# A two-layer hybrid trunk on one core: one flag on the tile context, so that the list scheduler chooses every engine's order over another machine model

## The chip, the core and the metric

One core of a Trainium2 chip runs the whole kernel. Its engines have a queue of instructions each and work through it strictly in the order in which the program puts them there: PE (TensorE, matrix products), DVE (VectorE), ACT (ScalarE), POOL (GpSimd) and SP (which here only issues DMAs). An instruction whose operands or whose target buffer are not ready holds up everything behind it on the same engine. The metric is device time in microseconds (us): the median of several executions.

## The reference, cut to what is computed

528 positions (512 and 16 learned ones ahead of them) of width 1024 pass two layers. Each layer has a token mixer and a gated feed-forward part with a short convolution, and a LayerNorm behind each of the four. The first mixer is a gated delta rule over 8 heads of width 128, in chunks:

```python
for i in range(DEPTH):                       # DEPTH = 2
    if i % 2 == 0:
        mix = gated_deltanet(h, ...)         # 8 heads, chunked
    else:
        mix = short_conv_mixer(h, ...)
    h = layer_norm(ALPHA * h + mix, ...)
    h = layer_norm(ALPHA * h + conv_ffn(h, ...), ...)

# inside gated_deltanet, for each head
u = solve(I + m, v_beta)                     # lower triangular, m from k, beta, decay
w = solve(I + m, k_beta * exp(g))
for each chunk i:                            # a chain from chunk to chunk
    v_new = u_i - w_i @ state
    o_i = qg_i @ state + qk_i @ v_new
    state = state * exp(gl_i) + kd_i.T @ v_new
```

## The kernel before

Everything is float32 and held transposed: `h` is 128 partitions by 8 strips by 528 positions. A large product is made of three products of rounded halves, high with high, high with low, low with high; the halves are called `hh`/`hl` for the activations and `wh`/`wl` for the weights:

```python
TE.matmul(ps, hi[:, k, :], r_h, ...)         # L278
TE.matmul(ps, hi[:, k, :], r_l, ...)         # L279
TE.matmul(ps, lo[:, k, :], r_h, ...)         # L280
```

The halves are made by `split`: ACT writes the high one (L88), DVE subtracts for the low one (L89). Weights come by DMA into `raw` tiles and are split just ahead of their use.

**The first stage (to about 380 us) is the gated delta rule.** It has two kinds of work on PE:

- *Projections* from `hh`/`hl` and the weights, lines L278 to L280: `psba` (decay and beta), `ps<head><group><half>` (k, v and q of a head, 144 matmuls for a head) and `psz<head><half>` (the output gate, 48 for a head). They hang on nothing but weights and a free buffer. ACT takes their results out of PSUM (L416/L417, or L624 for the gate), and DVE and ACT make the convolution and the activation; the buffers of these results are few (two PSUM banks, three or four tiles of each kind), so a projection can run ahead of the heads only so far.
- *The heads' own chains* of small dependent matmuls. `gdn_a` (L444 ff.) makes for each head transposes and products (`pk`, `pv`, `pn`, `pp`, `pq`, `psNb`), and then seven levels of a triangular inverse. A level is `p1` on PE (L508), ACT to `T` (L513), `p2` on PE (L519), DVE into `D` (L520), `pt` on PE (L524), ACT to `DT` (L525), and the next level's `p1`. Level 0 has no `p2`. `pr` (L534/L535), `pz` (L543/L544) and `py` (L550) refine the inverse. `gdn_b` is the recurrence over five chunks: `sa` on PE (L571), ACT to `vn` (L572), `sa` on PE (L575), DVE to the state `St` (L577/L579), `sa` and `sb` on PE (L566, L567), DVE to `rr` (L568), and L571 again. Then `po0` and `po` (L588, L585), a norm on ACT, DVE and POOL (L595 to L600), and `gdn_c`'s transpose `pot` (L610), after which the head's strip of `h` is ready.

Names such as `p263` are read as `p2`, head 6, level 3; `sa7` is head 7's recurrence. Two or three heads are in flight at once (recurrence of head i, levels of heads i+1 and i+2). The first product behind the stage is `pd0`, and it needs all of `h`, that is `pot7`.

**Behind it** come `down(0)` with a LayerNorm, the first feed-forward part (`ffn(1)`: `up`, `pairs`, `down(1)`), the short convolution (`short_conv`, with `down(2)`), the second feed-forward part and the final norm. A LayerNorm inside `down` goes in two halves of positions, because of what PE can do meanwhile: the first half's products `pd_<m>_0` come first, some of the second half's (`pd_<m>_1`) are held back, and the norm of the first half is to run beside them:

```python
for m in range(2, KD):
    together(go(m, 0))
    if m < keep:
        together(go(m, 1))
lnorm(idx, *rng[0], acc[0])
for m in range(keep, KD):
    together(go(m, 1))
lnorm(idx, *rng[1], acc[1])
```

In `lnorm` PE makes `mean` (L711), DVE subtracts it (L715), ACT squares (L717, L720), DVE adds (L721), PE makes `var` (L722), ACT a reciprocal root `r0` (L724), DVE refines it (L725 to L727) and multiplies (L732), ACT writes `hh` (L733) and `h` (L734), DVE `hl` (L735). The next products `pu` need `hh` and, one step on, `hl`. `var1_12` and `mean1_272` are of `down(1)`: its first half begins at position 12, its second at 272.

**What sets the order.** The code hands its instructions to the tile framework in an order that `weave` (L648), `staggered` and the held-back products lay out by hand. When the context closes, the framework's list scheduler goes through them with a model of the machine, and puts on each engine's queue what that model says is ready and first; it also decides there in which order buffers of one kind are given out, and so which semaphores an instruction waits for. Nothing else in the kernel fixes the order. The context is opened at L1207.

## Time and profile before

| | |
|---|---|
| median of 3 executions | 1331.18 us (1330.91 to 1331.32) |
| the profiled execution | 1330.96 us |
| its span on the core | 1329.2 us, so 1.8 us lie around it |
| granted TensorE clock, mean | 0.999 |
| matmuls in the profile, all engines' instructions | 10569, 26094 |
| first `pd0` (end of the first stage) | 379.69 us from the span's start |

A row of a window gives for each engine the time it was busy in that stretch and, after x, the number of instructions. A row of a timeline gives the start, the duration, the engine, the line, and the operation with its tiles (without their numbers); what stands in brackets is the idle time just before it and what ended it. Matmuls are pipelined, so the distance from one start to the next, and not the duration, is what a matmul costs on a full queue.

### The profile page before, as it was taken

To read this page: it belongs to the slowest core of one execution; us is meant where nothing else is said; L and a number is where in the kernel's file an instruction comes from. 1 tells how busy PE (TensorE), PEld (TensorE's weight loads), DVE (VectorE), ACT (ScalarE), POOL (GpSimd) and SP (SyncE) were. 2 spreads that over 40 slices of the span, in tenths; PEclk is the share of its full clock that TensorE was granted. 3 is DMA by queue.
4 is the path that set the end of the run, shared out by engine and by line. 5 is a ranking of instruction groups with operands and counts; after the bars stand their busy time and mean duration, and the time that the engine had idled before them with its cause. 6 is when DMAs were issued, how large, how long until landed. Compare 5 with 4: busy or idle time off the path is not lost.

```text
span 1329.2 us, 26094 instructions
## 1 busy us (share of the span) xinstructions
PE 1295.3 (97%) x10569; PEld 1244.6 (94%) x10569; DVE 1039.4 (78%) x1875; ACT 765.6 (58%) x1597; POOL 91.8 (7%) x132
## 2 busy tenths in 40 slices
PE   7999999999999999999999999999999999999997
PEld 6899989999999999999999999999998998998996
DVE  6667777776567898968959789889689796895987
ACT  5676767776454846626636566456377562662660
POOL 0322333311010000000000000000000000000000
PEclk9999999999999999999999999999999999999999
DMA  5111111111161142522422511423133242341331
GB/s 201 64 49 33 49 48 33 49 37 45 49 209 62 38 138 81 152 71 77 147 64 89 151 49 60 132 96 125 51 96 112 64 143 80 96 143 49 97 126 63
DMA packets 36185, 116.87 MB, mean 88 GB/s; under 512 B 4065, under 2 KB 5601, under 8 KB 36065
## 3 DMA queue, kind: packets, MB, share of 16 engines
q1 hardware_dynamic: 35280, 112.83, 27.4%
q0 software_dynamic: 640, 2.12, 0.5%
q8 instruction: 82, 1.34, 0.4%
q14 instruction: 39, 0.31, 0.1%
q10 hardware_dynamic: 144, 0.26, 0.1%
HBM read 113.10 MB, written 2.10 MB: 87 GB/s over the span
## 4 chain that ended last, share of the span: by engine, by line
PE 81%; DVE 10%; ACT 4%; issue 2%; POOL 2%; DMA 1%; SPq 0%; DVEq 0%; ACTq 0%; POOLq 0%
PE px L278 6%; PE px L280 6%; PE px L279 6%; PE pd L278 5%; PE pd L279 5%; PE pd L280 5%; PE pz L278 3%; PE pz L279 3%; PE pz L280 3%; PE pt L822 3%; PE pt L823 3%; PE pt L824 3%; PE pu L280 2%; PE pu L279 2%; PE pu L278 2%; PE ps L280 2%
## 5 line engine op out<-in xcount | busy, mean ns | idle before, releaser
L88 ACT ACTIVATE wh<-raw 128x512 fp32r<-128x512 f32 (+3 forms) x309 | 234.9, 767 | 187.5 <-PE pd L279 60.8
L89 DVE TENSOR_TENSOR wl<-raw,wh 128x512 fp32r<-128x512 f32 (+3 forms) x309 | 263.2, 862 | 60.9 <-ACT wh L88 60.0
L88 ACT ACTIVATE wh<-s 128x512 fp32r<-128x512 f32 x129 | 81.3, 630 | 100.1 <-PE pt L823 45.3
L278 PE MATMUL pd<-gh,wh 128*128 128x260 f32 (+2 forms) x480 | 135.5, 284 | 2.0 <-ACT gh L88 1.2
L279 PE MATMUL pd<-gl,wh 128*128 128x260 f32 (+2 forms) x480 | 135.4, 283 | 0.0
L280 PE MATMUL pd<-gh,wl 128*128 128x260 f32 (+2 forms) x480 | 134.9, 282 | 0.0
L279 PE MATMUL pu<-hl,wh 128*128 128x258 f32 (+3 forms) x400 | 114.4, 289 | 1.5 <-DVE hl L735 1.4
L278 PE MATMUL ps<-hh,wh 128*128 128x264 f32 x384 | 114.5, 299 | 0.9 <-ACT acc L417 0.9
L280 PE MATMUL ps<-hh,wl 128*128 128x264 f32 x384 | 115.3, 300 | 0.0
L279 PE MATMUL ps<-hl,wh 128*128 128x264 f32 x384 | 114.1, 297 | 0.0
L280 PE MATMUL pu<-hh,wl 128*128 128x258 f32 (+3 forms) x400 | 113.3, 288 | 0.5 <-DVE wl L89 0.5
L278 PE MATMUL pu<-hh,wh 128*128 128x258 f32 (+3 forms) x400 | 113.2, 288 | 0.0
L89 DVE TENSOR_TENSOR wl<-s,wh 128x512 fp32r<-128x512 f32 x129 | 88.7, 687 | 12.4 <-ACT wh L88 9.4
L278 PE MATMUL px<-sumh,wh 128*128 128x258 f32 (+1 forms) x344 | 97.6, 284 | 0.0
L280 PE MATMUL px<-sumh,wl 128*128 128x258 f32 (+1 forms) x344 | 97.5, 283 | 0.0
L278 PE MATMUL px<-hh,wh 128*128 128x258 f32 (+1 forms) x344 | 97.3, 283 | 0.0
L279 PE MATMUL px<-suml,wh 128*128 128x258 f32 (+1 forms) x344 | 97.3, 283 | 0.0
L280 PE MATMUL px<-hh,wl 128*128 128x258 f32 (+1 forms) x344 | 96.9, 282 | 0.0
L279 PE MATMUL px<-hl,wh 128*128 128x258 f32 (+1 forms) x344 | 96.9, 282 | 0.0
L278 PEld LDWEIGHTS pd<-gh,wh 128*128 128x128 f32 x480 | 90.1, 188 | 2.8 <-ACT gh L88 1.4
L279 PEld LDWEIGHTS pd<-gl,wh 128*128 128x128 f32 x480 | 90.5, 189 | 0.4
L280 PEld LDWEIGHTS pd<-gh,wl 128*128 128x128 f32 x480 | 90.5, 189 | 0.0
(315 smaller groups left out, 4098.3 us busy)
## 6 DMA issues: line engine op xcount, KB each, us to landing
raw<-in_w_up_dram SPq DMA_DIRECT2D x88, 512.0 KB, 3.7
raw<-in_w_bi_dram SPq DMA_DIRECT2D x24, 512.0 KB, 3.8
raw<-in_w_qkv_dram SPq DMA_DIRECT2D x23, 512.0 KB, 3.7
raw<-in_w_dt_dram SPq DMA_DIRECT2D x22, 512.0 KB, 4.5
raw<-in_w_dn_dram SPq DMA_DIRECT2D x24, 384.0 KB, 3.5
raw<-in_w_z_dram SPq DMA_DIRECT2D x8, 512.0 KB, 3.7
raw<-in_w_ao_dram SPq DMA_DIRECT2D x8, 512.0 KB, 3.7
raw<-in_w_bo_dram SPq DMA_DIRECT2D x8, 384.0 KB, 3.5
```

The source lines that it names most:

```text
L88: S.activation(hi, src, AF.Copy)
L89: V.tensor_tensor(lo, src, hi.bitcast(F32), ALU.subtract)
L278: TE.matmul(ps, hi[:, k, :], r_h, start=start and k == 0, stop=False, **kw)
L279: TE.matmul(ps, hi[:, k, :], r_l, start=False, stop=False, **kw)
L280: TE.matmul(ps, lo[:, k, :], r_h, start=False, stop=stop and k == nk - 1, **kw)
L822: TE.matmul(ps, gh[:, k, ts_], w_h, start=k == 0, stop=False)
L823: TE.matmul(ps, gl[:, k, ts_], w_h, start=False, stop=False)
L824: TE.matmul(ps, gh[:, k, ts_], w_l, start=False, stop=k == nk - 1)
```

## The change

```diff
--- before.py
+++ after.py
@@ -1204,7 +1204,7 @@
-    with tile.TileContext(nc) as tc:
+    with tile.TileContext(nc, schedule_with_timeline_sim=True) as tc:
         tile_hybrid_trunk(tc, *args)
```

The list scheduler now runs over its other model of the machine, the one that has engine queues. The instructions that compute and the DMAs are the same ones; the order on the queues and the waits differ. On PE 8251 of 11274 instructions stand at another place: up to 1086 places away in the first stage, about 100 at most behind it. The queue that issues the DMAs moves by five places or fewer. ACT has 415 instructions that only wait for semaphores where there were 348, PE 33 where there were 24.

The first place is PE's queue in the middle of head 7's recurrence, `sa7`, near the end of the first stage. Before:

```order
L571 MATMUL sa7_4446<-rr7_4445,DT7_3961 106x128
L279 MATMUL psz40_4754<-hl_69,wh0_82 128x260
L280 MATMUL psz40_4754<-hh_68,wl0_83 128x260
L278 MATMUL psz41_4780<-hh_68,wh0_82 128x258
L279 MATMUL psz41_4780<-hl_69,wh0_82 128x258
L575 MATMUL sa7_4446<-vn7_4442,kd7_3962 128x128
L280 MATMUL psz41_4780<-hh_68,wl0_83 128x258
L278 MATMUL psz41_4780<-hh_68,wh0_82 128x258
L279 MATMUL psz41_4780<-hl_69,wh0_82 128x258
L280 MATMUL psz41_4780<-hh_68,wl0_83 128x258
L278 MATMUL psz41_4780<-hh_68,wh0_82 128x258
L566 MATMUL sa7_4446<-St7_4444,qkv7_1_3740 106x128
```

The same queue now, from the first `sa7` on:

```order
L571 MATMUL sa7_4446<-vb7_3963,DT7_3961 106x128
L575 MATMUL sa7_4446<-vn7_4442,kd7_3962 128x128
L610 MATMUL pot6_4459<-cst_sb_71,oS6_4256 128x106 x5
L566 MATMUL sa7_4446<-St7_4444,qkv7_1_3740 106x128
L567 MATMUL sb7_4447<-St7_4444,qkv7_0_3738 106x128
L571 MATMUL sa7_4446<-rr7_4445,DT7_3961 106x128
L575 MATMUL sa7_4446<-vn7_4442,kd7_3962 128x128
L566 MATMUL sa7_4446<-St7_4444,qkv7_1_3740 106x128
L567 MATMUL sb7_4447<-St7_4444,qkv7_0_3738 106x128
L571 MATMUL sa7_4446<-rr7_4445,DT7_3961 106x128
L575 MATMUL sa7_4446<-vn7_4442,kd7_3962 128x128
```

The gate's projections that stood between the links of the chain have moved ahead of it, and the links stand one behind the other.

The second place is PE's queue at the variance of the first half in `down(1)`. Before, `var1_12` stands in the middle of a held-back strip (`pd1_4_1`), with the rest of it and strips 5 to 7 of the second half behind it:

```order
L280 MATMUL pd1_4_1_98_9753<-gh_5023,wl0_83 128x256
L278 MATMUL pd1_4_1_98_9753<-gh_5023,wh0_82 128x256
L722 MATMUL var1_12_9620<-acc1_0_9419,onesm_76 128x260
L279 MATMUL pd1_4_1_98_9753<-gl_5024,wh0_82 128x256
L280 MATMUL pd1_4_1_98_9753<-gh_5023,wl0_83 128x256
```

Now it stands behind the last held-back strip, `pd1_7_1`, with the mean of the second half and the next stage's products right behind it:

```order
L279 MATMUL pd1_7_1_98_9816<-gl_5024,wh1_5015 128x256
L280 MATMUL pd1_7_1_98_9816<-gh_5023,wl1_5016 128x256
L722 MATMUL var1_12_9620<-acc1_0_9419,onesm_76 128x260
L711 MATMUL mean1_272_9837<-acc1_1_9420,onesm_76 128x256
L278 MATMUL pu99_0_0_9929<-hh_68,wh1_5015 128x258
L278 MATMUL pu100_1_0_9933<-hh_68,wh1_5015 128x258
```

The variance has moved behind all of the second half's products, and nothing but the second mean stands between it and the products that need the norm.

The third place is ACT's queue at the same norm, behind its reciprocal root `r01_12`. Before:

```order
L724 ACTIVATE r01_12_9652<-var1_12_9620,epsc_132 128x260
L88 ACTIVATE wh0_82<-raw120_9490 128x1024
L88 ACTIVATE wh0_82<-raw121_9911 128x1024
L733 ACTIVATE hh_68<-h_67,par_sb_70 128x260 x2
L734 ACTIVATE h_67<-h_67,par_sb_70 128x260 x2
```

And now:

```order
L724 ACTIVATE r01_12_9652<-var1_12_9620,epsc_132 128x260
L717 ACTIVATE acc1_1_9420<-h_67 128x256
L720 ACTIVATE s2_1_272_1_9843<-h_67 128x256
L720 ACTIVATE s2_1_272_2_9847<-h_67 128x256
L720 ACTIVATE s2_1_272_3_9851<-h_67 128x256
L720 ACTIVATE s2_1_272_4_9855<-h_67 128x256
L720 ACTIVATE s2_1_272_5_9859<-h_67 128x256
L733 ACTIVATE hh_68<-h_67,par_sb_70 128x260 x2
```

The second half's squares have moved ahead of the first half's output; on DVE the subtractions that feed them (L715, eight of them) stand ahead of L732 in the same way. `down(0)` and `down(2)` show the same three moves.

## The prediction

> **What bounds the kernel now.** I read the page first, for the shares and the chain of work that ended last:
>
> ```profile
> span 1329.2 us, 26094 instructions
> PE 1295.3 (97%) x10569; PEld 1244.6 (94%) x10569; DVE 1039.4 (78%) x1875; ACT 765.6 (58%) x1597; POOL 91.8 (7%) x132
> PE 81%; DVE 10%; ACT 4%; issue 2%; POOL 2%; DMA 1%; SPq 0%; DVEq 0%; ACTq 0%; POOLq 0%
> ```
>
> PE is busy for 97% of the span, and four fifths of the chain lie on it. The change adds and removes no instruction that computes, so it can gain only from PE's gaps, and lose wherever it opens new ones. The busy time by windows says where the gaps are:
>
> ```profile
> 0.00:33.00 33.00, 24.14 (x165) 20.87 (x166) 20.55 (x58) 18.35 (x35) 2.50 (x23) 1.00 0.59 202
> 200.00:300.00 100.00, 96.32 (x943) 91.60 (x941) 73.66 (x128) 72.83 (x196) 26.48 (x27) 1.00 0.15 43
> 300.00:380.00 80.00, 76.30 (x701) 72.10 (x701) 45.00 (x82) 43.03 (x114) 8.52 (x9) 1.00 0.17 49
> 500.00:600.00 100.00, 100.00 (x834) 99.76 (x834) 80.97 (x138) 52.66 (x97) 0.00 (x0) 1.00 0.32 98
> 782.00:802.00 20.00, 19.60 (x161) 19.30 (x160) 18.37 (x47) 13.01 (x28) 0.00 (x0) 1.00 0.36 110
> ```
>
> The first figure behind the length is PE. Behind the first stage it has no gap (500 to 600: 834 matmuls, 0.12 us each). In the first stage it loses under 4%, though there it runs chains of small dependent matmuls. At a LayerNorm (782 to 802) it loses 0.4 of 20 us. PE's waits, grouped by what ended them, are short:
>
> ```profile
> PE psba L278 <- ACT hh L88: 7.4, 2, 4.8
> PE sa L566 <- DVE St L579: 3.0, 4, 1.0
> PE pot L610 <- DVE oS L600: 2.5, 2, 1.5
> ```
>
> The largest is the start. The dependent steps wait little because projections stand between them, as the rows of the first place in the section on the change show. So the question is what happens to each dependent step when the order changes.
>
> **What a dependent step costs when nothing covers it.** From PE's timeline near the end of the first stage:
>
> ```profile
> 335.19 0.41 PE L508 MATMUL p<-D,N 106*106 106x106 f16 x5
> 336.37 0.41 PE L519 MATMUL p<-T,DT 106*106 106x106 f16 x5
> 337.58 0.44 PE L524 MATMUL pt<-ident,D 106*106 106x106 f16 x5
> 338.73 0.21 PE L534 MATMUL pr<-D,N 106*106 106x106 f16 x1
> 341.36 0.25 PE L543 MATMUL pz<-DT,N 106*106 106x106 f16 x1
> 342.48 0.28 PE L280 MATMUL psz<-hh,wl 128*128 128x258 f32 x1
> 342.94 0.21 PE L543 MATMUL pz<-DT,N 106*106 106x106 f16 x1
> 342.99 0.21 PE L544 MATMUL pz<-DT,L 106*106 106x106 f16 x1
> 343.02 0.37 PE L278 MATMUL psz<-hh,wh 128*128 128x258 f32 x1
> 343.22 0.28 PE L279 MATMUL psz<-hl,wh 128*128 128x258 f32 x1
> 347.15 0.41 PE L571 MATMUL sa<-vb,DT 106*106 106x128 f32 x2
> 354.70 0.49 PE L575 MATMUL sa<-vn,kd 106*128 106x128 f32 x2
> 355.62 0.47 PE L566 MATMUL sa<-St,qkv 128*106 128x128 f32 x2
> 356.54 0.47 PE L571 MATMUL sa<-rr,DT 106*106 106x128 f32 x2
> 357.46 0.49 PE L575 MATMUL sa<-vn,kd 106*128 106x128 f32 x2
> 361.02 0.38 PE L588 MATMUL po<-vn,PT 106*106 106x128 f32 x2
> 361.27 1.12 PE L585 MATMUL po<-vn,PT 106*106 106x128 f32 x8
> 367.58 0.67 PE L610 MATMUL pot<-cst_sb,oS 106*128 106x106 f32 x5 [1.48 <-DVE oS L600]
> ```
>
> These are head 7's last steps. A **level step** (L508, L519, L524, L534) comes 1.15 to 1.21 us after the one before: 1.2. A **recurrence step** (L575, L566, L571, L575) comes every 0.92. From `pr` to the first `sa` there are 8.42 us with projections put between; taking those out I choose 7 (estimate; the two shortest of its three gaps, 2.6 and 1.3, stay). From `po0` to `pot` there are 6.56. On the engine itself a half-precision matmul costs 0.05 (342.94 to 342.99), a float32 one about 0.2 (four in 361.27's 1.12, less its tail), and a projection 0.12, the first behind small ones 0.20 (343.02 to 343.22), so a break costs 0.05 to 0.08.
>
> **The first stage, term by term.** PE's new queue up to `pot7` holds the same 1584 projection matmuls and 1464 small ones, but the projections stand in 81 runs where there were 229, and all of them stand ahead of `pot7` (90 stood behind it). They run far ahead: 864 are queued, to head 5's v strip `ps521`, before head 0's level 5. Then they are held by their buffers, and the queue has long stretches of small matmuls alone. I cut it in stretches with projections (F) and without (E).
>
> The seven F stretches: 1584 × 0.122 = 193, their 425 small matmuls 49 at the prices above, 74 breaks × 0.05 = 4. The first 33 us stay as they are: 165 matmuls that would take 20 take 33, so 13 more. Sum **259**; these stretches wait for nothing.
>
> The E stretches run at the pace of their chains. Where a level of one head and a recurrence step of another alternate in the queue, as they do nearly everywhere, both go at the slower one's 1.2:
>
> - E1 (`pt04` to `po00`): 7 level steps 8.4, `pr` to `sa` 7, 12 recurrence steps 14.4: 29.8
> - E2 (in head 1's recurrence, up to `ps600`): 8 steps, 9.6
> - E3 (`pt26` to `po02`): 1.2 + 7 + 14.4 = 22.6
> - E4 (two pieces around `psz50`/`psz51`): 5, and 3 steps with `pr` to `sa` 10.6: 15.6
> - E5 (`sa4` to `po05`): 21 recurrence steps 25.2, and some 6 for eight groups of five float32 matmuls among them: 31
> - E6 (`pt65` to `pot7`): 4 steps 4.8, 7, 14.4 for `sa6`, 3.4 from `po06` to `sa7`, 12 × 0.92 = 11 for `sa7` alone, 1 for `po`, 6.6: 48.2
>
> That is 157. The same prices make 25.6 of before's stretch from 338.73 to 367.58 (7 + 11 + 1 + 6.6), which took 28.85, 1.13 times as long. I take 157 × 1.13 = 177. The stage then ends at 259 + 177 = 436 instead of 379.7: **+56**. The lower bound has each recurrence at 0.92 throughout and no 1.13: 65 steps × 0.28 = 18 less, 139, so +18. For the upper bound two chains that share a queue wait for each other's ACT and DVE work as well; 1.3 times 157 is 204, so +83.
>
> **The three LayerNorms in `down`.** Before, at the second:
>
> ```profile
> 777.94 0.60 PE L722 MATMUL var<-acc,onesm 128*128 128x260 f32 x2
> 782.12 0.41 DVE L756 TENSOR_TENSOR h<-h,pd 128x256 f32<-128x256 f32 x1
> 782.45 0.42 DVE L727 SCALAR_TENSOR_TENSOR r<-s,r 128x260 f32<-128x260 f32 x1
> 784.28 1.09 ACT L733 ACTIVATE hh<-h,par_sb 128x260 fp32r<-128x260 f32 x2
> 785.23 0.28 PE L280 MATMUL pd<-gh,wl 128*128 128x256 f32 x1
> 785.35 0.63 PE L278 MATMUL pu<-hh,wh 128*128 128x258 f32 x4
> 786.38 0.39 PE L279 MATMUL pu<-hl,wh 128*128 128x258 f32 x1 [0.40 <-DVE hl L735]
> ```
>
> From `var` to the first `pu` go 7.41 us, and held-back `pd` fill them to 785.23. In the new order nothing is left for that (second place of the change). Counted from the last `pd`: DVE adds it to `h` and closes the sums, five instructions 0.34 apart and a hop, so `var` at 2.3; the root `r0` done at 3.3 behind a `var` and an ACTIVATE; then 13 DVE instructions to L732 (L725 to L727, two L721, and the eight L715 of the other half), 4.4, so 7.8; `hh` one L732 and one ACTIVATE (0.55 of the pair's 1.09) later, at 8.7; `hl` behind eight L732 and an L721, at 11.3. PE has the two norm matmuls and six `pu` to do in that, about 1.3: **10 us idle at each, +30**. Lower bound: the 7.41 of before less a mean matmul's 0.6, 6.8 each, +20. Upper: DVE also has one or two splits of weights there (1.2 each in the same timeline), 12.7 each, +38.
>
> **The rest.** Behind the first stage nothing else moves more than about 100 places on PE, and I found two places where a matmul stands closer to its producer than before (in the first strip of `down(0)`, and at `ph1`): 3, between 0 and 8. The DMA queue moves by five places or fewer, and DMA is busy 15 to 36% of the windows above behind the start: 0. The 67 added waits on ACT stand on work that the E stretches already count.
>
> Sum: 1331 + 56 + 30 + 3 = **1420 us**. The profiled execution's 1330.96 is 0.2 under the median, which changes nothing.
>
> [...] The startup shows PE at another pace:
>
> ```profile
> 10.34 0.40 PE L278 MATMUL psba<-hh,ba_hi 128*16 128x264 f32 x1 [2.59 <-ACT hh L88]
> 14.74 0.42 PE L280 MATMUL ps<-hh,wl 128*128 128x264 f32 x1
> 14.96 0.42 PE L278 MATMUL psba<-hh,ba_hi 128*16 128x264 f32 x1
> 15.69 0.28 PE L280 MATMUL psba<-hh,ba_lo 128*16 128x264 f32 x1
> ```
>
> Behind the idle time the matmuls start 0.22 apart until 15 us, then 0.12, while the granted clock of that window is shown as 1.00. [...]
>
> **The rivals.**
>
> - *The slow pace of the start comes back* where PE is thin. For it: PE's own work in the E stretches (1039 small matmuls at the prices above) is 101 of 177 us, and the rows of the start. Against it: no gap inside an E stretch is longer than some 2 us. Price: at 0.22 for 0.12 that work takes 0.83 × 101 = 84 more, of which waits hide some 30, with 5 behind the norms: 1420 + 59 = 1479. [...] Chance 0.15.
> - *The chains go at their bare prices*, and DVE and ACT, free of projections, are early: +18 to +25 and +20 at the norms, so 1370 to 1378. For it: ACT and DVE are below 75% in the stage. Chance 0.2.
> - *Not slower.* 148 fewer breaks × 0.05 to 0.08 gain 7 to 12 us, already in my sum. If the chains of two or three heads hid each other, so that the E stretches took PE's own work of 101, the stage would end at 360 and gain 20; with norms that cost 7 in all, 1331 − 20 + 7 = 1318. It decides if the E stretches take less than 380 − 259 − 7 = 114 us in all, 13 more than PE's own work. Against it: the last `sa7` steps have nothing beside them, and their chain alone takes 19 us (11 + 1 + 6.6) for some 4 of work. Chance 0.04.
> - That nothing changes is excluded by the two orders.
>
> **How the numbers follow.** Forecast 1395 to 1450, chance 0.55; the rest (0.06) is worse than 1485. The range 1370 to 1485 takes both bounds of the two large terms (1331 + 18 + 20 = 1369; 1331 + 83 + 38 + 8 = 1460, and the slow pace above it). About 0.2%, 2.7 us, is what a measurement of this kernel can tell from no change. Faster by more than that 0.04, within 0.02, slower 0.94.
>
> **What would show it.** PE's busy share in the windows of the first stage falls from 96% to below 80% between 140 and 420 us, and stays near 96% ahead of 138; the first `pd0` starts near 436. New PE waits of the kind "`sa` L575 for ACT `vn`", "`p` L519 for ACT `T`", "`pt` L524 for DVE `D`" sum to 60 us or more. Three idles near 10 us stand ahead of `pu` (waiting for `hh` L733 and `hl` L735), and the windows away from them hold 834 matmuls in 100 us as before. Projections 0.22 apart in F stretches would show the slow pace. The forecast is wrong if the busy share of the first stage stays above 90%, or if `var` at the norms doesn't stand idle before the next `pu`.

## The result: 1453 us, 9.1% slower

| | before | after |
|---|---|---|
| median | 1331.25 us (1330.91 to 1332.26, 4 runs) | 1453.17 us (1450.79 to 1454.75, 4 runs) |
| ratio | | 1.0914 (95% interval 1.0901 to 1.0927) |
| span of the profiled execution | 1329.2 us | 1451.1 us |
| first `pd0`, end of the first stage | 379.7 us | 460.3 us |
| from there to the end of the span | 949.5 us | 990.8 us |
| mean granted TensorE clock | 0.999 | 0.942 |

The forecast was 1420 us in a range of 1370 to 1485. Of the 121.9 us that the span grew, 80.6 lie in the first stage and 41.3 behind it. The page of the changed kernel, its first lines and the rows of PE and its granted clock in 40 slices:

```profile
span 1451.1 us, 26169 instructions
PE 1347.8 (93%) x10569; PEld 1287.9 (89%) x10569; DVE 1047.1 (72%) x1875; ACT 773.1 (53%) x1597; POOL 86.7 (6%) x132
PE   7999888998777979999999997999979999999997
PEclk9999897998955989999999998999979999999999
```

DVE and ACT are busy for as long as before to within 1%, so the work is the same; PE, with as many matmuls, is busy for 52 us longer and still only 93% of the span. The clock row says how both can be: in before every slice had a 9, and here eight slices are lower: five in the first stage (slices 5 to 13, down to 5) and one at each of the three LayerNorms in `down` (slices 15, 25 and 30). PE's waits, grouped by what ended them (us in total, times, longest):

```profile
PE pu L278 <- ACT hh L733: 15.9, 3, 5.6
PE var L722 <- DVE acc L721: 11.2, 3, 4.8
PE p L519 <- ACT T L513: 5.7, 14, 0.8
PE pt L524 <- DVE D L520: 5.5, 11, 1.2
PE p L508 <- ACT DT L525: 4.9, 10, 1.5
PE sa L575 <- ACT vn L572: 3.3, 7, 0.7
```

The first two are the three norms, 27 us. The others are links of the heads' chains, which hardly waited before. Stretches of the first stage, as the prediction cut them (E1, F2, E3, E5, E6; PE's busy time and count first, the granted clock behind POOL):

```profile
134.80:171.90 37.10, 29.38 (x265) 25.12 (x262) 21.01 (x40) 23.38 (x55) 9.45 (x13) 0.77 0.05 15
171.90:195.40 23.50, 23.44 (x214) 23.44 (x215) 15.49 (x27) 13.15 (x42) 3.87 (x6) 1.00 0.16 46
233.90:266.50 32.60, 25.63 (x205) 22.19 (x205) 17.41 (x33) 19.45 (x49) 10.02 (x13) 0.74 0.06 17
352.50:389.80 37.30, 29.87 (x280) 24.95 (x279) 26.51 (x54) 20.68 (x71) 8.29 (x8) 1.00 0.06 15
396.20:460.30 64.10, 45.34 (x265) 36.36 (x263) 26.11 (x50) 24.92 (x64) 8.38 (x11) 0.54 0.12 38
```

F2 is full: 23.44 of 23.5 us. The E stretches hold 265 matmuls in 37 us or in 64, and in all of these but E5 the clock is down. Head 7's recurrence lies in the last of them; PE's timeline shows one of its chunks:

```profile
443.63 0.79 PE L575 MATMUL sa<-vn,kd 106*128 106x128 f32 x2 [0.46 <-ACT vn L572]
444.86 0.76 PE L566 MATMUL sa<-St,qkv 128*106 128x128 f32 x2 [0.44 <-DVE St L579]
446.06 0.76 PE L571 MATMUL sa<-rr,DT 106*106 106x128 f32 x2
447.28 0.80 PE L575 MATMUL sa<-vn,kd 106*128 106x128 f32 x2 [0.46 <-ACT vn L572]
```

It takes 3.65 us, where before's took 2.76 with projections between its links, and each row of two matmuls lasts 0.76 to 0.80 where it lasted 0.47 to 0.49.

### The profile page after: what moved, and what is told of

The parts are those of the page before. It is cut to its first block, busy times and chain, and to the rows that moved or that the text cites. A ratio compares the mean times of both kernels' runs of the same rounds, so it can differ in the third digit from the quotient of the medians.

```text
span 1451.1 us, 26169 instructions
## 1 busy us (share of the span) xinstructions
PE 1347.8 (93%) x10569; PEld 1287.9 (89%) x10569; DVE 1047.1 (72%) x1875; ACT 773.1 (53%) x1597; POOL 86.7 (6%) x132
## 4 chain that ended last, share of the span: by engine, by line
PE 84%; DVE 7%; ACT 5%; issue 2%; DMA 1%; POOL 0%; SPq 0%; DVEq 0%; ACTq 0%; POOLq 0%
PE px L280 6%; PE px L279 6%; PE px L278 6%; PE pd L278 5%; PE pd L279 5%; PE pd L280 5%; PE pu L279 4%; PE pu L280 4%; PE pu L278 3%; PE ps L278 3%; PE ps L280 3%; PE ps L279 3%; PE pz L280 3%; PE pz L278 3%; PE pz L279 3%; PE pt L822 3%
## 5 line engine op out<-in xcount | busy, mean ns | idle before, releaser
L278 PE MATMUL pd<-gh,wh 128*128 128x260 f32 (+2 forms) x480 | 130.3, 282 | 3.0 <-ACT gh L88 3.0
L278 PE MATMUL pu<-hh,wh 128*128 128x258 f32 (+3 forms) x400 | 113.6, 301 | 15.9 <-ACT hh L733 15.9
L279 PE MATMUL pu<-hl,wh 128*128 128x258 f32 (+3 forms) x400 | 118.9, 298 | 2.3 <-DVE hl L735 2.3
L280 PE MATMUL pu<-hh,wl 128*128 128x258 f32 (+3 forms) x400 | 117.7, 295 | 0.0
L88 ACT ACTIVATE wh<-s 128x512 fp32r<-128x512 f32 x129 | 80.7, 626 | 68.6 <-PE pd L279 22.8
L280 PE MATMUL ps<-hh,wl 128*128 128x264 f32 x384 | 111.1, 290 | 0.0
L279 PE MATMUL ps<-hl,wh 128*128 128x264 f32 x384 | 110.7, 289 | 0.0
L278 PEld LDWEIGHTS pu<-hh,wh 128*128 128x128 f32 x400 | 76.7, 201 | 18.5 <-ACT hh L733 17.8
```

What stands on the lines that cost most here:

```text
L88: S.activation(hi, src, AF.Copy)
L278: TE.matmul(ps, hi[:, k, :], r_h, start=start and k == 0, stop=False, **kw)
L279: TE.matmul(ps, hi[:, k, :], r_l, start=False, stop=False, **kw)
L280: TE.matmul(ps, lo[:, k, :], r_h, start=False, stop=stop and k == nk - 1, **kw)
```

## The experiments

Where nothing else is said, each starts from the changed kernel. An edge between two instructions below orders them on their engine's queue and makes neither wait for the other's end. The scheduler chooses everything that has no edge anew, so each run has its own orders on the other queues too. `behind` gives such edges to all instructions of the same engine traced since a mark:

```python
def behind(tc, n0, ins):
    for i in traced(tc)[n0:]:
        if i.engine == ins.engine:
            tc.add_manual_dep(i, ins.name, ORDER, reason="order")   # ORDER: NoSync
```

| run | median us | end of the first stage | from `mean` of `down(1)`'s first half to its `pu` |
|---|---|---|---|
| before | 1331.3 | 379.7 | 14.8 |
| after | 1453.2 | 460.3 | 21.7 |
| e1 norm, PE | 1448.9 | 461.6 | 19.8 |
| e2 paced projections | 1408.7 | 419.2 | 22.2 |
| e3 e1 and e2 | 1407.7 | 418.9 | 19.5 |
| e4 added work, `sa`'s bank | 1453.5 | 460.1 | 22.2 |
| e5 norm, PE and DVE | 1446.9 | 461.7 | 19.5 |
| e6 other pacing | 1433.1 | 441.4 | 21.7 |
| e7 e5 and e6 | 1426.3 | 436.1 | 18.7 |
| e8 added work, own bank | 1453.0 | 460.3 | 22.2 |
| e9 before's PE order, first stage | 1410.8 | 421.3 | 21.7 |
| e10 before's PE order | 1409.5 | 421.7 | 21.5 |
| e11 before's DVE order | 1503.1 | 498.2 | 13.9 |
| e12 before's PE and DVE order | 1412.2 | 404.9 | 14.8 |

### e1 and e5: the norms

e1 moves only PE's held-back strips:

```diff
         lnorm(idx, *rng[0], acc[0])
         for m in range(keep, KD):
-            together(go(m, 1))
+            queued(tc, lambda: together(go(m, 1)), MARK[idx] if m > 4 else None)
```

`MARK[idx]` is the first half's `var`, and `queued` gives `behind` to what it traces.

> The changed kernel, in which the held-back strips 5 to 7 of each LayerNorm in down are queued on PE behind the variance of the first half, about where before had them; nothing else is touched. Theory (the norm's place on PE's queue costs 34 us: some 26 of idle PE at the three norms and some 8 at a lower granted clock behind them): 1453 - 33 = 1420 us, between 1414 and 1426; PE's waits for hh L733 and for acc L721 fall from 15.9 and 11.2 us to under 3 each, and the granted clock from 500 us on stays at 1.00. Rival (only the wait that the profile puts on L733 goes, and DVE's queue still holds hl back): 1437 us or more.

It gained 4.3 us, not 33. The wait for `hh` went (15.9 to 2.5 us), but the one of `var` grew from 11.2 to 18.2: PE now arrives earlier at a variance that isn't ready. The rival's number holds, though not its reason: it is `var` that is late, not `hl`. Why stands in DVE's timeline of the changed kernel behind `mean` (at 869.76):

```profile
875.27 0.41 DVE L721 TENSOR_TENSOR acc<-acc,s 128x260 f32<-128x260 f32 x1
875.61 0.41 DVE L760 TENSOR_TENSOR acc<-acc,h 128x256 f32<-128x256 f32 x1
875.95 0.41 DVE L756 TENSOR_TENSOR h<-h,pd 128x256 f32<-128x256 f32 x1
876.28 1.21 DVE L89 TENSOR_TENSOR wl<-raw,wh 128x1024 fp32r<-128x1024 f32 x1
877.41 0.41 DVE L721 TENSOR_TENSOR acc<-acc,s 128x260 f32<-128x260 f32 x1
```

and what follows from it in PE's:

```profile
869.76 0.60 PE L711 MATMUL mean<-acc,onesm 128*128 128x260 f32 x2
884.72 0.70 PE L722 MATMUL var<-acc,onesm 128*128 128x260 f32 x2 [2.88 <-DVE acc L721]
891.43 1.66 PE L278 MATMUL pu<-hh,wh 128*128 128x258 f32 x6 [5.57 <-ACT hh L733]
```

Between two of the seven additions L721 that the variance needs, DVE makes a sum of the second half (L760, L756) and often a split of weights of 1.2 us. So the time from `mean` to `var` is 15.0 us. Before it was 7.4 (770.53 to 777.94), and no split stood among the seven additions, the first of which began at 772.62 and the last at 777.16:

```profile
770.53 0.71 PE L711 MATMUL mean<-acc,onesm 128*128 128x260 f32 x2
```

e5 therefore adds an edge on DVE: the sums of the strips m > 2, and the splits traced with them, go behind the last L721.

```diff
-            queued(tc, lambda: together(go(m, 1)), MARK[idx] if m > 4 else None)
+            queued(tc, lambda: together(go(m, 1)), *(held if m > 4 else held[1:] if m > 2 else ()))
```

> The changed kernel with e1's edit on PE, and on DVE too the sums of the held-back strips 3 to 7 (L756, L758, L760, and the weight splits issued with them) queued behind the last L721 of the first half's norm. Theory (the norm is late because DVE alternates each L721 with the second half's sums and with splits of 1.2 us: 14.9 us from mean to var where before has 7.4): mean to var falls to 9 us or less, PE's idle time at the three norms together to 5 us or less, the granted clock behind them stays at 1.00, total 1453 - 30 = 1423 us, between 1416 and 1431. Rival (ACT's squares, one of which waits for each L721 and for splits of its own, hold var back): mean to var stays above 12 us, total above 1440.

From `mean` to `var` it went down to 9.0, 10.2 and 10.7 us, near the bound expected, and yet the total fell by 6 us only, 2 us more than in e1, which is little beside the spread of the runs (1444.9 to 1448.5). So the theory's total didn't come out (1416 to 1431), and the rival's did (above 1440) without its condition (above 12 us). PE waits 15.6 us for the three variances:

```profile
PE var L722 <- DVE acc L721: 15.6, 3, 6.2
```

In this order `mean` itself stands later: 47 held-back matmuls of `down(1)` are ahead of it where before has 27, and with e5 there are 43 left between `mean` and `var`, 5.2 us at 0.12, against before's 58. A part of the cover had been used up earlier, and no edge at `var` brings it back. That this is what was missing isn't shown: e10 below puts the 58 back in their place, and `var` still waits 12.0 us.

### e2, e6, e3 and e7: the projections

e2 ties each projection to a link of the chains. `STEPS` holds the last PE instruction of each step of the round of heads that was traced ahead of it, 48 steps of a projection are spread evenly over them, and the gates' 128 over the last three rounds:

```diff
-                drain(proj(hd + 3, res[hd + 3]))
+                drain(paced(tc, proj(hd + 3, res[hd + 3]), 0, 48))
...
-            drain(gate(hd))
+            drain(paced(tc, gate(hd), 16 * hd, 16 * NH, False))
```

> The changed kernel, in which each projection of the first stage may be queued on PE only behind a link of the heads' chains: the 48 steps of a head's projection are spread evenly over the links of the round of heads ahead of it, and the gates over the last three rounds. Theory (the first stage lost 81 us because projections were used up early, several us at a time for each link, so that later links had nothing beside them): the stage ends at 385 to 395 us instead of 460, granted clock 1.00 there, total 1453 - 70 = 1383 us, between 1372 and 1392. Rival (the order on ACT and DVE, or the latency of the links in this order, costs it, and not what PE has to do meanwhile): the stage ends above 430 us, total above 1420.

Why the projections are used up early is seen in the changed kernel's first stretch, where head 0's level 1 goes through PE:

```profile
86.50 0.41 PE L524 MATMUL pt<-ident,D 106*106 106x106 f16 x5
91.01 0.41 PE L508 MATMUL p<-D,N 106*106 106x106 f16 x5
94.48 0.41 PE L519 MATMUL p<-T,DT 106*106 106x106 f16 x5
98.67 0.41 PE L524 MATMUL pt<-ident,D 106*106 106x106 f16 x5
```

A link that can follow in 1.2 us comes after 3.5 to 4.5, since some 30 projections were queued between: ACT had `T` for the third row ready at 92.06 (it starts at 91.45 and takes 0.61), and PE came to it at 94.48. That work was missing later.

With e2's edges the projections stand in 221 runs (81 after, 229 before). The stage ends at 419 us and the total falls by 44 us: 41 of the stage's 81 us are back, less than the theory wanted and more than the rival allowed. The middle rounds are as short as before's: from `po01` to `po03` 80.8 us, before 78.7, after 106.5. The other 40 us are lost at both ends, 24 by `po01` and 13 from `po03` on, where the even spread leaves links without cover. That this is what costs them isn't shown: e9 below, with before's own order on PE, ends the stage no earlier.

> The changed kernel with a pacing of the projections that differs from e2's at both ends: the first projections of each head may go 6 to 24 steps ahead, and of the gates' 128 steps 24, 34 and 34 stand in the last three rounds and 36 behind head 7's last product. Theory (e2 recovered the middle rounds, 40 us a round as before, and lost 18 us in the first two rounds and 12 in the last two for want of projections): the stage ends between 388 and 402 us, total 1385 us, between 1374 and 1397. Rival (what e2 left is not PE's cover but the order on ACT and DVE in this model): the stage ends above 410 us, total within 8 us of e2's 1409.

e6 let the projections go 6 steps ahead (24 and 8 in the first two) and moved some gates behind the end:

```diff
-            behind(tc, n0, steps[min(i * len(steps) // n, len(steps) - 1)])
+        if i >= lead:
+            behind(tc, n0, steps[min((i - lead) * len(steps) // 48, len(steps) - 1)])
```

The expectation failed: the stage ends 22 us later than e2's, and the middle rounds take 91.9 us. A lead of 6 steps out of 48 means that the last eighth of a round's links has no projection left, and each round pays 5 us for it. The trace agrees: from 199.0 to 203.8 us and from 204.6 to 210.4 e6 has small matmuls alone on PE, and the mean granted clock of the whole run is 0.954 where e2 has 0.972. The places of the gates were changed in the same run and weren't tried alone.

> The changed kernel with both edits, the norms' strips behind the variance and the projections paced along the chains. Theory (two places carry the whole loss and don't touch each other): 1453 - 33 - 70 = 1350 us, between 1338 and 1360, so at most 2% above before. Rival (the new order costs all over the kernel, on ACT and DVE as well): 1375 us or more.

> The changed kernel with the edits of e5 and e6 together. Theory (the first stage's projections and the norms' sums carry all of the loss): 1385 - 30 = 1355 us, between 1343 and 1367, within 3% of before. Rival (much is lost elsewhere): above 1375.

e3 comes to 1407.7 and e7 to 1426.3 us: the edits of the norms add 1 and 7 us to those of the stage. Both expectations, which added up the theories of the parts, were 58 and 71 us too low.

### e4 and e8: the clock

Work is added between the links of a recurrence, two matmuls of a constant each time:

```diff
-                TE.matmul(sa[:CH, 1, :], DT[:, c, :], r_, start=True, stop=True)
+                TE.matmul(sa[:CH, 1, :], DT[:, c, :], r_, start=True, stop=True); hot(tc, sa[:, 3, :], onesm, hd)
```

> The changed kernel with work added: behind each L571, L575 and L567 of the recurrences of heads 6 and 7 stand two more float32 matmuls of a constant into an unused quarter of sa's bank, 78 or so in all, which nobody reads. Theory (PE's clock was granted at half there because PE had little to do, and slows the links themselves): the granted clock between 400 and 460 us rises from 0.54 to above 0.9, sa7's recurrence from its first L571 to po07 falls from 15.8 us to 12.5 or less, total 1446 us or less although PE does more. Rival (links wait for ACT and DVE only, the clock doesn't matter): the recurrence takes 15.8 us or more, total 1453 to 1465.

The expectation failed: from 400 to 460 us the mean granted clock was 0.81, head 7's recurrence took 18.7 us, and the total didn't move. The clock was at 1.00 from 440 to 450 us, and yet a chunk there took 4.4 us. ACT's timeline shows that it waited for the added matmuls too, which wrote into the bank that it reads:

```profile
442.32 0.37 ACT L572 ACTIVATE vn<-sa,rk 106x128 f32<-106x128 f32 x1 [2.92 <-PE sa L1266]
```

L1266 is the added matmul, and it writes another part of the bank than ACT reads. So e4 says nothing of the links' length, and e8 repeats it for head 7 with a bank of its own:

```diff
-                TE.matmul(sa[:CH, 1, :], DT[:, c, :], r_, start=True, stop=True); hot(tc, sa[:, 3, :], onesm, hd)
+                TE.matmul(sa[:CH, 1, :], DT[:, c, :], r_, start=True, stop=True); hot(tc, dm[:, 0, :], onesm, hd)
```

> The changed kernel with work added in head 7's recurrence alone, two float32 matmuls of a constant behind each L571, L575 and L567 as in e4, but into a bank of their own, which no other engine reads (in e4 they wrote into the bank that ACT and DVE read, and the links took longer although the clock was back at 1.00). Nobody reads them. Theory (at half the clock a link takes 1.22 us, at the full clock 0.9): the granted clock from the second chunk on is above 0.9, and a chunk of three links takes 2.9 us or less instead of 3.65. Rival (links have the same length at any clock): a chunk takes 3.5 us or more. The total says little, since head 6's last transpose moves behind the recurrence: 1448 to 1455.

PE's timeline of e8, links and added matmuls of one chunk:

```profile
444.54 0.49 PE L575 MATMUL sa<-vn,kd 106*128 106x128 f32 x2
444.86 0.61 PE L1266 MATMUL dm<-onesm 128*128 128x128 f32 x4
445.47 0.47 PE L566 MATMUL sa<-St,qkv 128*106 128x128 f32 x2
445.77 0.38 PE L567 MATMUL sb<-St,qkv 128*106 128x128 f32 x2
445.99 0.61 PE L1266 MATMUL dm<-onesm 128*128 128x128 f32 x4
446.44 0.41 PE L571 MATMUL sa<-rr,DT 106*106 106x128 f32 x2
446.69 0.61 PE L1266 MATMUL dm<-onesm 128*128 128x128 f32 x4
447.31 0.49 PE L575 MATMUL sa<-vn,kd 106*128 106x128 f32 x2
```

And the window around it, with the granted clock behind POOL:

```profile
438.00:450.00 12.00, 11.98 (x80) 10.90 (x79) 2.74 (x8) 1.45 (x4) 0.00 (x0) 0.85 0.00 0
```

A chunk takes 2.77 us instead of 3.65, with more work in it. The windows ahead of it, from 425 to 438 us, show 0.50, so the 0.85 is half the clock until an estimated 441.6 us and the full one behind it. The chunk ahead of the full clock (`sa` L575 at 437.70 to the next at 441.79), with the same matmuls added, took 4.09. The theory held for this chain: its links wait for the clock, 0.88 us or 24% of a chunk. The total didn't move, as expected: the first third of the recurrence still ran at half speed until the clock rose, and the last transpose of head 6 came later.

### e9 to e12: whole queues pinned to before's order

Each instruction of a queue gets an edge to the one that stood ahead of it in before's program (a table of names), and the scheduler places the other engines around it:

```diff
-        tile_hybrid_trunk(tc, *args)
+        tile_hybrid_trunk(tc, *args); follow(tc, PE_ORDER)
...
+        for a, b in zip(names, names[1:]):
+            tc.add_manual_dep(by[b], a, info, reason="order")
```

> The changed kernel with PE's queue up to the first pd0 pinned to the order that before had; DVE, ACT and POOL, and all that comes behind, stay with the new scheduler's choice. Theory (the first stage's 81 us come from PE's order alone, and e2 and e6 fell short because an even spread isn't before's): the stage ends between 380 and 393 us with the granted clock at 1.00, total 1331 + 34 for the norms + some 8 = 1373 us, between 1364 and 1384. Rival (the orders of ACT and DVE carry a part): the stage ends above 405 us, total above 1390.

With PE's queue of the first stage exactly before's, the stage ends at 421.3 us, where e2 had it. That isn't the theory's 380 to 393, and the rival is right that other engines carry a part. Nor are the 39 us that came back a share of PE's alone, since ACT's and DVE's orders were chosen anew around the pinned queue.

> The changed kernel with the whole of PE's queue pinned to before's order; DVE, ACT and POOL stay with the new choice. Theory (e1 and e5 had too little of the second half left between mean and var: 19 to 43 held-back matmuls where before has 54 to 58; with those and the 56 to 63 behind var in place, only DVE's own order is left, about 3 us at each norm): total 1331 + 8 + 9 = 1348 us, between 1336 and 1358. Rival (DVE's order makes the norms late whatever PE does): the norms still cost 20 us or more, total above 1362.

The total stays where e9 has it (1409.5), and the norm of `down(1)` still takes 21.5 us from `mean` to `pu`. PE's waits show that this isn't for nothing:

```profile
PE var L722 <- DVE acc L721: 12.0, 3, 4.7
PE pd L278 <- ACT gh L88: 9.3, 3, 3.7
```

The waits for `hh`, 15.9 us in e9, are gone, and with those for `hl` the norms cost PE 15.7 us of waiting in place of 29.4. What that gains is lost again elsewhere behind the stage: 6.6 us of it are the waits for `gh` (2.7 in e9), and the rest isn't traced. So half of the norms' waiting hangs on PE's order. Most of the other half is `var`, which DVE makes late, as the rival said (e12, with DVE's order too, has no wait for it). The rival's total came out; its 20 us at the norms did not.

> The changed kernel with DVE's queue pinned to before's order and PE, ACT and POOL left to the new choice (PE's norms then have 75 held-back matmuls between mean and var and 16 to 23 behind var). Theory (the first stage hangs on PE's order and not on DVE's): the stage ends within 10 us of 460; the norms lose half of their 34 us; total 1435 us, between 1422 and 1448. Rival (DVE's order matters in the first stage): the stage ends below 440 us, total below 1420.

Before's DVE order alone brings the norms to 13.7 to 14.1 us and makes the kernel 50 us slower than the change did, 38 of them in the first stage. Neither theory nor rival had this: an order of DVE that is good beside before's PE is bad beside the PE order that the new model chooses around it.

> The changed kernel with PE's and DVE's queues pinned to before's order; only ACT, POOL and the DMA issues keep the new choice. Theory (PE's order carries the first stage, PE's and DVE's the norms, ACT's nothing): 1334 us, between 1329 and 1340. Rival (ACT's order costs by itself): 1345 us or more.

With both, the norms take as long as before's from `mean` to `pu` (14.3, 14.8 and 15.2 us) and the stage is down to 404.9, but the total is 1412. The granted clock is 1.00 in the stage from 33 us on, so the 25 us that are left aren't the clock's: PE has 133 matmuls behind it at 33 us where before it had 165, and from there to the end of the stage it is idle for 33 us where before it was for 13. The waits are for ACT first:

```profile
PE sa L575 <- ACT vn L572: 6.6, 6, 1.8
PE p L519 <- ACT T L513: 4.9, 6, 1.5
PE p L508 <- ACT DT L525: 4.3, 5, 1.3
```

One of them in ACT's timeline. PE issued the level's `p1` at 130.65:

```profile
130.98 1.08 ACT L88 ACTIVATE wh<-raw 128x1024 fp32r<-128x1024 f32 x1
131.93 0.41 ACT L416 ACTIVATE cb<-ps 128x264 f32<-128x264 f32 x1
132.20 0.51 ACT L417 ACTIVATE acc<-ps,par_sb 128x264 f32<-128x264 f32 x1
132.57 0.31 ACT L491 ACTIVATE sqa<-pq 106x128 f32<-106x128 f32 x1
132.72 0.25 ACT L491 ACTIVATION_READ_ACCUMULATOR sqa<-pq 106x1 f32 x1
132.82 0.66 ACT L513 ACTIVATE T<-p 106x530 f16<-106x530 f32 x1
```

ACT has a split of weights and a projection's copies queued ahead of `T`, and PE's next step waits 1.45 us for it. Behind the stage e12 loses 58 us to before, more than the change's 41 although its norms are as long as before's; the largest wait there is one that neither kernel shows among its own, PE's `pz` for DVE's `pu` (L1017), 18.7 us in 12 places. So e12 prices what ACT, POOL and the buffers cost beside before's PE and DVE, and not their share in the changed kernel, whose ACT queue is another one. The expectation was wrong by 78 us.

No version beat before.

## Why the prediction was right, and where it wasn't

**The direction and the size** came from the E stretches and the norms, and both are where the loss is: 80.6 us in the stage (forecast 56, between 18 and 83) and 41.3 behind it, of which the three norms make 34 (forecast 30); the remaining 7 are small drifts and the first 5.7 us of `pd0`, at half clock (forecast 3). Within the stage the number is closer than the mechanism, as follows.

**F stretches.** Forecast 259 us, measured 252.9 (134.8 for the first with its start, and 23.5, 22.8, 48.4, 7.1, 9.9 and 6.4). They wait for nothing, as the row of F2 shows.

**E stretches.** Forecast 157 × 1.13 = 177, measured 37.1, 15.7, 32.6, 20.6, 37.3 and 64.1, together 207.4: 1.32 times the bare prices. The step that was mis-sized is the factor 1.13, which came from a stretch at full clock. The rival *the slow pace of the start comes back* got 0.15, with the argument that no gap would be longer than 2 us. The gaps are indeed short, 1.7 us at most but for the 5.3 ahead of `pot7`, and the clock fell all the same. What the prediction had as 101 us of PE's own work and 76 of waits came out as 157 busy and 50 idle, summed over the pieces (a row of two matmuls in the chunk above counts as busy for 0.76 to 0.80 of the 1.20 to 1.23 us to the next row). So the waits were priced too high and PE's own matmuls, which it took at their full-clock prices, too low, and that the sum came within 30 us is in part luck. By the granted clock of their windows the E stretches spent 110 us at half (46% of E1, 44% of E2, 52% of E3, 64% of E4's second piece, 92% of E6); at e8's 24%, which is measured on one chain only, that is an estimated 26 us, most of the 30 missing. E5, with PE 80% busy, kept the full clock and came out at 1.20. The rival's own price of 59, with 5 of it behind the norms, was too high: the same estimate makes 26 here and some 7 there.

**That the stage's cost comes from the order of PE's queue** was half right. Two independent edits of PE's queue, e2 and e9, bring back 39 to 41 of the 81 us. Pinning DVE as well brings 17 more, though pinning DVE alone costs 38, so these aren't shares that add up. The last 25 remain with ACT's and POOL's orders, or the buffers and semaphores that come with them. With all queues pinned nothing was tried, so these aren't told apart and that part of the cause stays open; the waits and the timeline of e12 point at ACT.

**The norms.** Forecast 10 us idle each, measured 8.7, 8.5 and 10.0, and the three lose some 7 more to the clock behind them (34 less 27): it is at half for 13.6, 13.6 and 17.1 us there. No run shows the 5 us that the price of the slow pace has behind the norms; these 7 are what was measured in their place. The size was right, and the second part of the cause too: nothing is left to cover the way from `var` to `pu`, 6.7 us in the row. The first part was only half the cause. I had `var` at 2.3 us behind the last `pd` and put the delay down to PE's place for it and to the eight L715 ahead of L732. But `var` is late from above: DVE's additions alternate with other work all the way from `mean`. Giving `var` its place back on PE leaves it waiting (18.2 us for the three in e1, 12.0 in e10), and PE's whole order back (e10) halves the waiting of the norms; with DVE's order as well (e12) no wait for `var` is left.

**"The 67 added waits on ACT stand on work that the E stretches already count"**, and with it ACT's cost of nothing, was the weakest sentence. ACT is 53% busy, and yet with PE's and DVE's orders as before the kernel is still 81 us behind. How much of the changed kernel's own loss is ACT's no run tells.

**The signs.** PE is busy for 102 of the 105 us from 33 to 138, the norms have their three idles near 10 us, and away from them 100 us hold 822 to 836 matmuls. But between 138 and 420 us PE's busy share is 87%, not below 80%, the first `pd0` starts at 460 and not near 436, and the three waits that were to sum to 60 us or more sum to 14.5. These miss for the reason given under the E stretches: more of the loss is PE at half clock, which the profile counts as busy, and less of it waiting.

**The rival that ends on the other side** (fewer breaks) was nowhere near: the breaks it saves are in the F stretches, 6 us better than forecast.

## What to carry to other kernels

Cover is a stock: a schedule that fills a link of 1.2 us with 3.5 us of independent work pays later with links that have nothing beside them, so count what is left for the last chain. The orders of the engines are one plan: one engine's good order, pinned beside another plan's orders, can be worse than either plan (e11), and the best partial repair here won 45 of the 122 us. And a chain with little beside it is to be priced at half-clock links too, not only at those that the profile of a full engine shows: E6 had half the clock in 59 of its 64 us, E5 in none of its 37.

## What the runs showed of the hardware

The clock fell at 138.3 us in the changed kernel, with no gap of PE above 0.92 us in the 3 us ahead of it. In windows (PE's busy time, and the granted clock behind POOL):

```profile
134.80:138.00 3.20, 1.79 (x28) 1.49 (x26) 2.50 (x4) 3.01 (x6) 0.00 (x0) 1.00 0.01 3
138.00:141.00 3.00, 2.69 (x25) 2.23 (x25) 1.42 (x2) 1.36 (x3) 0.00 (x0) 0.55 0.52 175
...
150.00:153.00 3.00, 2.07 (x16) 1.84 (x16) 1.78 (x3) 2.23 (x4) 0.00 (x0) 0.50 0.00 0
153.00:156.00 3.00, 3.00 (x23) 2.90 (x21) 0.35 (x2) 1.95 (x6) 1.81 (x2) 0.60 0.00 0
156.00:160.00 4.00, 2.79 (x28) 2.18 (x26) 2.40 (x6) 2.98 (x13) 1.20 (x1) 1.00 0.00 0
```

PE was 56% busy in the 3.2 us of the first row; then the clock stayed at half for 15 us at 69 to 90% busy, and it came back at 155.4 us, within 3 us in which PE had no gap. The trace's record of the clock has stretches at half of 17.1, 6.8, 17.1, 13.6 and 64.9 us that begin in the first stage, and of 13.6, 13.6 and 17.1 us at the three norms. What brings the clock down isn't shown: E5, at 80% busy, had 1.00 for all of its 37 us.
